# The last four k-tiles of the first layer's shift and scale, summed on VectorE instead of TensorE

## The chip, the cores and the metric

The kernel runs on one core of one Trainium2 chip. The metric is the device time of one execution in microseconds (us), median of the runs shown; the profile is of one further execution. A core has TensorE (PE in the rows; its weight loads are PEld), VectorE (DVE), ScalarE (ACT), GpSimd (POOL) and SyncE (SP), whose queue issues the DMAs that this text is about.

## What is computed

The reference is a two-layer attention block on 256 latent and 256 context tokens of width 2048, followed by one more block (a mixer, a cross-attention and a feed-forward part), all in fp32. The change touches only how each of the first block's two layers gets its modulation. For layer 0:

```python
sc, scc = jax.nn.silu(c), jax.nn.silu(c_ctx)                       # two vectors of 2048
shift, scale, gate = jnp.split(sc @ w_ada[l] + b_ada[l], 3, axis=-1)        # w_ada[l]: 2048 x 6144
shift_c, scale_c, gate_c = jnp.split(scc @ w_ada[l] + b_ada[l], 3, axis=-1)
h = rms(x, norm_w[l]) * (1.0 + scale[:, None]) + shift[:, None]
hc = rms(xc, norm_w[l]) * (1.0 + scale_c) + shift_c
u = h @ w_in[l]                                                    # and hc @ w_in[l]
```

So no product with `w_in` can use a column of `h` before the shift and the scale of that column are there, and these are sums over 2048 rows of `w_ada`.

## The kernel before

**Tiling.** All 512 tokens stand in four tiles of 128 (two latent, two context; t = 0 to 3). The width 2048 is 16 k-tiles of 128 columns. A product with `w_in` for one chunk of 512 output columns, one token tile and one k-tile is three TensorE instructions, since each fp32 factor is split in a rounded part `hi` and a rest `lo` (hi·hi, hi·lo, lo·hi; lines 481 to 483). Weights come by 512 KB loads of two k-tiles (line 448, three `raw` buffers); ScalarE makes each `hi` (line 420) and VectorE each `lo` (line 421), four buffers of each.

**The first products.** `first_products` works through the first three chunks of `w_in` in five parts of the k-tiles, `PARTS`: 0-1, 2-3, 4-7, 8-11, 12-15. I call them parts 0 to 4. In part i all three chunks are multiplied by the k-tiles of that part: 72 products in parts 0 and 1, 144 in each of parts 2 to 4. A chunk has four PSUM banks, one for each token tile, and there are four such banks in all (`psum`, tag d), so a bank is free for the next chunk only when its sums have been moved out: by copies in part 0 (line 408 or 414), by VectorE adds to the earlier parts' sums from part 1 on (line 1403, tiles `va` and `a`).

**Columns of the modulation.** While part i is multiplied, `ada_pe` makes shift and scale of part i+1. It loads the columns of `w_ada` that this part needs (8.4 MB for four k-tiles, 32 loads of 256 KB, line 694; eight buffers, shared tags P and PT) and multiplies them by the two silu vectors, eight groups of four matmuls with 32 columns of weights (line 698, tile `adao`). Its `end` copies the sums out (705), turns them by four transposes (708, `adat`), adds the pieces (712, `adaT`), finishes them (664 to 666) and calls `done`, which makes the next activations: for each k-tile four transposes of x (530), two VectorE multiplications (540, `h`), two ScalarE shifts (543), `hi` (545) and `lo` (546). Two PSUM banks serve these transposes, so the transposes of one k-tile wait until the multiplications of the k-tile two before it are done.

**The other form.** `ada_steps` does such sums on VectorE, for the gates and for layer 1: weights laid out by column, so that a row of 512 products lies in a partition; a step loads two 256 KB tiles (line 736, three `raw2` buffers) and for each of two streams makes one multiplication with a running sum (line 739, SCALAR_TENSOR_TENSOR and a read of the accumulator). The silu vector, spread over all partitions, is a tile `cb` (line 732, two buffers). Before the change this starts after the first products.

**What sets the order.** The program is written in one stream of operations; jobs are taken up by a clock of expected TensorE time (`tick`, `push`, `side_rate`), and a scheduler then puts each engine's instructions in a fixed order. Each engine runs its list strictly in order, and so does SP's queue: an issue that waits for a buffer holds those behind it.

Of the kernel before, what the change touches and what calls it, by code (L numbers as in the profile page):

```python
# [132 lines left out]
def packed_ada(w):  # L133


    x = w[0].reshape(16, 128, 3, D)
    out = [x[:, :, :2, 128 * k0:128 * (k0 + n)].ravel() for k0, n in PARTS]
    for l, a, b in ((0, 2, 3), (1, 0, 2), (1, 2, 3)):
        out.append(w[l][:, a * D:b * D].reshape(4, 512, -1, 128).transpose(0, 2, 3, 1).ravel())
    return np.concatenate(out)  # L140
# [499 lines left out]
class Block1(K):  # L640
# [27 lines left out]
    def ada_pe(self, k0, n, cst, done):  # L668
# [11 lines left out]
        def step(kt0):  # L680
# [15 lines left out]
            for kt, b in reversed(raws):  # L696
                q = 64 * (kt % 2) + 32 * b
                m = nc.tensor.matmul(acc[q:q + 32, :W], lhsT=cst[:, kt, :], rhs=raws[kt, b], start=kt < 2,
                                     stop=kt >= NKT - 2, skip_group_check=True)
                if (kt, b) != (kt0 + 1, 1):  # L700
                    self.tc.keep_in_program_order(m)
# [16 lines left out]
    def ada_steps(self, l, b0, nb, streams):  # L718
# [3 lines left out]
        w, ns, n = self.a["w_ada"], len(streams), 16 * nb  # L722
        st = {}
        at0 = w.offset + ((0 if l == 0 else 16) + (0 if l == 0 else 16 * b0)) * D * 128 + 2 * D * D
# [19 lines left out]
        def end():  # L744
            t = self.ada_tile(l)
            for b in range(nb):
                nc.vector.tensor_reduce(t[:, b0 + b, :ns], st["p"][:, :, 16 * b:16 * b + 16], op=OP.add, axis=AX.X)
            if b0 == 0:
                self.finish_ada(l, 0, 16)
# [632 lines left out]
    def first_products(self, h, w, chunks):  # L1382
# [4 lines left out]
        def steps(i):  # L1387
            k0, n = PARTS[i]

            def done():  # L1390
                h.limit = k0 + n
                h.need(k0 + 1)
            return self.ada_pe(k0, n, self.cst, done)

        h.need(1)
        self.side_rate = self.rates["first"]
        for i, (k0, n) in enumerate(PARTS):
            if i + 1 < len(PARTS):
                for f in steps(i + 1):
                    self.push(f)  # L1400
            self.every = n * len(chunks) * 2.56 / FIRST
# [6 lines left out]
    def block1(self):  # L1408
        nc, a, tc = self.nc, self.a, self.tc
        with ExitStack() as es:  # L1410
# [19 lines left out]
            self.cst = self.B("cstat", tag="cb").rearrange("p (k m) -> p k m", m=32)  # L1430
            nc.vector.memset(self.cst, 0.0)
            nc.vector.tensor_copy(self.cst[:, :, 0:2], self.cv.rearrange("p s k -> p k s"))
# [32 lines left out]
            self.rates = dict(first=0, vb=0.2, b=0.2, z=0.2, cq=0.2, ckv=0.2, c=0, out=0.2)  # L1465
# [537 lines left out]
```

## Time and profile before

| | us |
|---|---|
| median of 3 runs | 3488.35 |
| lowest, highest | 3487.48, 3488.5 |
| the profiled execution | 3488.5 |
| its span in the profile | 3486.4 |
| part 0 to part 4 of the first products, in the span | 35.4 to 219.0 |

The span leaves out 2.1 us of the execution's time around it. In rows of the timeline the columns are the start, the length, the engine, the line, the operation, the tiles (written<-read), the shape and the count, and in brackets the idle time before and what ended it. In a table of stretches each engine has its busy time and its count of instructions; then come the granted TensorE clock (1.00 is 2.4 GHz), the mean busy share of the 16 DMA engines and what they moved in GB/s. Consecutive instructions overlap, so what one costs in a row of its kind is the distance between two starts.

### The profile page before, as it was taken

The page shows a single profiled execution, that of the slowest core. Times are in us where ns is not written, and L with a number is a line of the kernel's source. Part 1 is how long each engine was busy: PE and PEld are TensorE (multiplying, and loading weights), DVE is VectorE, ACT ScalarE, POOL GpSimd, SP SyncE. Part 2 cuts the span into 40 slices and gives each one's busy share as a digit, 9 for nine tenths or more (in the row PEclk, how much of TensorE's full clock was granted, in tenths as well). Part 3 has the DMA queues.
Part 4 walks back from the last instruction along what each step waited for, and adds up shares of the span by engine and source line. Part 5 has one row for each costly group of instructions (what it writes and reads, how often), then busy time and mean ns, then how long its engine had stood idle before and what let it go on. Part 6 is the DMA issues. An engine that isn't in the chain of part 4 may idle for free. (4 is left out here: it accounts for less than half of the span.)

```text
span 3486.4 us, 57207 instructions
## 1 busy us (share of the span) xinstructions
PE 3360.5 (96%) x20842; PEld 2937.7 (84%) x20842; DVE 2296.0 (66%) x4939; ACT 1786.5 (51%) x3556; POOL 318.3 (9%) x472
## 2 busy tenths in 40 slices
PE   7999999999999998999999999999999899999998
PEld 4577778788787887887778999999888899999886
DVE  3488988778866576887664555555666766666554
ACT  3345655246335355756464445444556555555544
POOL 0022220112120121021200000000000000000000
PEclk9999999999999999999999999999999999999999
DMA  8845445642565434444644535555655455555554
GB/s 305 279 125 150 132 142 150 201 133 85 179 212 159 162 96 146 141 157 129 187 135 158 187 122 182 183 185 184 197 179 168 146 183 184 184 182 194 193 192 164
DMA packets 226778, 590.46 MB, mean 169 GB/s; under 512 B 39904, under 2 KB 63184, under 8 KB 226496
## 3 DMA queue, kind: packets, MB, share of 16 engines
q1 hardware_dynamic: 221104, 570.41, 51.2%
q0 software_dynamic: 4864, 15.69, 1.4%
q8 instruction: 164, 2.69, 0.3%
q14 instruction: 118, 0.97, 0.1%
q10 hardware_dynamic: 528, 0.71, 0.1%
HBM read 582.48 MB, written 4.24 MB: 168 GB/s over the span
## 5 line engine op out<-in xcount | busy, mean ns | idle before, releaser
L421 DVE TENSOR_TENSOR lo<-raw,hi 128x512 fp32r<-128x512 f32 (+3 forms) x1788 | 1206.3, 679 | 867.1 <-ACT hi L420 859.5
L420 ACT ACTIVATE hi<-raw 128x512 fp32r<-128x512 f32 (+3 forms) x1788 | 1089.7, 614 | 1254.3 <-PE upd L504 192.6
L502 PE MATMUL upd<-hi,hi 128*128 128x256 f32 x1408 | 399.1, 284 | 0.0
L504 PE MATMUL upd<-lo,hi 128*128 128x256 f32 x1408 | 398.9, 283 | 0.0
L505 PE MATMUL upd<-hi,lo 128*128 128x256 f32 x1408 | 398.7, 283 | 0.0
L739 DVE SCALAR_TENSOR_TENSOR scr<-raw,cb 128x512 f32<-128x512 f32 x448 | 298.2, 691 | 34.9 <-DMA raw<-in_w_ada_dram 17.6
L504 PEld LDWEIGHTS upd<-lo,hi 128*128 128x128 f32 x1408 | 270.7, 192 | 0.3 <-DVE lo L546 0.3
L505 PEld LDWEIGHTS upd<-hi,lo 128*128 128x128 f32 x1408 | 270.6, 192 | 0.0
L502 PEld LDWEIGHTS upd<-hi,hi 128*128 128x128 f32 x1408 | 270.6, 192 | 0.0
L399 POOL TENSOR_TENSOR sm<-sm,mhalf 128x2 f32<-128x2 f32 (+4 forms) x116 | 117.2, 1012 | 1407.4 <-DVE sm L398 1402.0
L481 PE MATMUL downd<-hi,hi 128*128 128x512 f32 x352 | 137.7, 391 | 0.0
L483 PE MATMUL downd<-hi,lo 128*128 128x512 f32 x352 | 137.7, 391 | 0.0
L482 PE MATMUL downd<-lo,hi 128*128 128x512 f32 x352 | 137.6, 391 | 0.0
L602 ACT ACTIVATE P<-Ss,sm 128x512 f32<-128x512 f32 (+1 forms) x164 | 99.6, 608 | 69.2 <-DVE sm L598 51.1
L408 ACT ACTIVATE PT<-pTt 128x256 f32<-128x256 f32 x226 | 79.3, 381 | 64.5 <-PE pTt L619 55.2
L481 PE MATMUL L0outd<-hi,hi 128*128 128x512 f32 x256 | 101.2, 395 | 4.3 <-DVE ot L1361 3.0
L502 PE MATMUL L0zd<-hi,hi 128*128 128x512 f32 x256 | 100.6, 393 | 1.4 <-DVE kpe L414 1.4
L505 PE MATMUL L0zd<-hi,lo 128*128 128x512 f32 x256 | 100.4, 392 | 1.0 <-DVE lo L421 0.9
L598 DVE TENSOR_REDUCE sm<-Ss 128x1 f32<-128x512 f32 (+1 forms) x164 | 95.1, 585 | 7.8 <-PE Ss L591 6.8
L483 PE MATMUL L0outd<-hi,lo 128*128 128x512 f32 x256 | 99.8, 392 | 0.3 <-DVE lo L421 0.3
L482 PE MATMUL L0outd<-lo,hi 128*128 128x512 f32 x256 | 100.0, 391 | 0.0
L504 PE MATMUL L0zd<-lo,hi 128*128 128x512 f32 x256 | 100.0, 391 | 0.0
(568 smaller groups left out, 8920.1 us busy)
## 6 DMA issues: line engine op xcount, KB each, us to landing
raw<-in_w_in_dram SPq DMA_DIRECT2D x344, 512.0 KB, 3.5
raw<-in_w_ada_dram SPq DMA_DIRECT2D x384, 256.0 KB, 3.4
raw<-in_ffn_w_up_dram SPq DMA_DIRECT2D x176, 512.0 KB, 3.5
raw<-in_w_out_dram SPq DMA_DIRECT2D x104, 512.0 KB, 4.1
raw<-in_ffn_w_down_dram SPq DMA_DIRECT2D x88, 512.0 KB, 3.8
raw<-in_w_proj_b_dram SPq DMA_DIRECT2D x32, 512.0 KB, 3.5
raw<-in_w_in_dram SPq DMA_DIRECT2D x32, 288.0 KB, 3.3
raw<-in_w_proj_a_dram SPq DMA_DIRECT2D x16, 512.0 KB, 3.7
```

What stands on the lines that cost most here:

```text
L399: nc.gpsimd.tensor_tensor(r, ms, self.mhalf[:, :n], op=OP.pow)
L420: self.nc.scalar.activation(hi, src, AF.Copy)
L421: self.nc.vector.tensor_sub(lo, src, hi.bitcast(F32))
L481: nc.tensor.matmul(ps[t][:, a], lhsT=xh, rhs=hi[:, a], start=first, stop=False)
L482: nc.tensor.matmul(ps[t][:, a], lhsT=xh, rhs=lo[:, a], start=False, stop=False)
L483: nc.tensor.matmul(ps[t][:, a], lhsT=xl, rhs=hi[:, a], start=False, stop=last)
L502: nc.tensor.matmul(p, lhsT=hi[:, s], rhs=xh, start=kt == 0 and c % per == 0, stop=False, skip_group_check=True)
L504: nc.tensor.matmul(p, lhsT=hi[:, s], rhs=xl, start=False, stop=False, skip_group_check=True)
L505: nc.tensor.matmul(p, lhsT=lo[:, s], rhs=xh, start=False, stop=kt == nk - 1, skip_group_check=True)
L598: nc.vector.tensor_reduce(nm[:, 0:1], S[:, :nk], op=OP.max, axis=AX.X, negate=True)
L602: nc.scalar.activation(P[:, :nk], S[:, :nk], AF.Exp, bias=nm[:, 0:1], accum_out=nm[:, 1:2])
L739: nc.vector.scalar_tensor_tensor(self.temp("scr"), raw, 1.0, st[s], op0=OP.mult, op1=OP.mult, accum_out=st["p"][:, s, k, q:q + 1])
```

## The change

Shift and scale of part 4 (k-tiles 12 to 15) are no longer made by `ada_pe` during part 3 but by `ada_steps`: `packed_ada` lays their weights out by column, `ada_steps` gets a first k-tile `k0` and a call `done`, and its 16 steps run as side work at a rate of 0.2 a microsecond of the clock from part 0 on; what is left of them is issued in one go at the start of part 3, except the last, which follows 20 us later and calls `done`. The constant `cst` becomes two tiles under another tag, because `cb` now holds the silu vectors from the start.

```diff
@@ packed_ada
     x = w[0].reshape(16, 128, 3, D)
-    out = [x[:, :, :2, 128 * k0:128 * (k0 + n)].ravel() for k0, n in PARTS]
-    for l, a, b in ((0, 2, 3), (1, 0, 2), (1, 2, 3)):
-        out.append(w[l][:, a * D:b * D].reshape(4, 512, -1, 128).transpose(0, 2, 3, 1).ravel())
+    out = [x[:, :, :2, 128 * k0:128 * (k0 + n)].ravel() for k0, n in PARTS[:-1]]
+    k0 = PARTS[-1][0]
+    for y in (w[0][:, 2 * D:], w[1][:, :2 * D], w[1][:, 2 * D:], x[:, :, :2, 128 * k0:].reshape(D, -1)):
+        out.append(y.reshape(4, 512, -1, 128).transpose(0, 2, 3, 1).ravel())
     return np.concatenate(out)
@@ ada_steps
-    def ada_steps(self, l, b0, nb, streams):
+    def ada_steps(self, l, b0, nb, streams, k0=0, done=None):
-        w, ns, n = self.a["w_ada"], len(streams), 16 * nb
+        nk = 16 - k0
+        w, ns, n = self.a["w_ada"], len(streams), nk * nb
         st = {}
-        at0 = w.offset + ((0 if l == 0 else 16) + (0 if l == 0 else 16 * b0)) * D * 128 + 2 * D * D
+        at0 = w.offset + 2 * D * 128 * PARTS[-1][0]
+        at0 += D * 128 * (64 if k0 else 0 if l == 0 else 16 + 16 * b0)
@@ ada_steps, end
-                nc.vector.tensor_reduce(t[:, b0 + b, :ns], st["p"][:, :, 16 * b:16 * b + 16], op=OP.add, axis=AX.X)
+                nc.vector.tensor_reduce(t[:, b0 + b, :ns, k0:], st["p"][:, :, nk * b:nk * b + nk], op=OP.add, axis=AX.X)
             if b0 == 0:
-                self.finish_ada(l, 0, 16)
+                self.finish_ada(l, k0, nk)
+                if done:
+                    done()
@@ first_products
-            return self.ada_pe(k0, n, self.cst, done)
+            if i + 1 < len(PARTS):
+                return self.ada_pe(k0, n, self.cst, done)
+            return self.ada_steps(0, 0, 2, [0, 1], k0, done)

         h.need(1)
         self.side_rate = self.rates["first"]
+        later, self.side = self.side, steps(len(PARTS) - 1)
+        last = self.side.pop()
         for i, (k0, n) in enumerate(PARTS):
-            if i + 1 < len(PARTS):
+            if i + 2 < len(PARTS):
                 for f in steps(i + 1):
                     self.push(f)
+            elif self.side is not later:
+                self.flush_side()
+                self.push(20.0)
+                self.push(last)
+                self.side = later
+                self.side_rate = 0
@@ block1
-            self.cst = self.B("cstat", tag="cb").rearrange("p (k m) -> p k m", m=32)
-            nc.vector.memset(self.cst, 0.0)
-            nc.vector.tensor_copy(self.cst[:, :, 0:2], self.cv.rearrange("p s k -> p k s"))
+            self.cst = []
+            for i in range(2):
+                x = self.B("cstat", tag="cqx", bufs=4, cols=256).rearrange("p (k m) -> p k m", m=32)
+                nc.vector.memset(x, 0.0)
+                nc.vector.tensor_copy(x[:, :, 0:2], self.cv[:, :, 8 * i:8 * i + 8].rearrange("p s k -> p k s"))
+                self.cst.append(x)
-            self.rates = dict(first=0, vb=0.2, b=0.2, z=0.2, cq=0.2, ckv=0.2, c=0, out=0.2)
+            self.rates = dict(first=0.2, vb=0.2, b=0.2, z=0.2, cq=0.2, ckv=0.2, c=0, out=0.2)
```

**Where the instructions come to stand.** The line numbers of the changed kernel are two to six, later sixteen, higher in this region (540 is 542, 739 is 743, 1403 is 1419). On TensorE the eight groups, the four transposes and their copy are gone from part 3. Elsewhere the order moves too; two places matter.

The first is VectorE's list around the start of part 3, after the multiplications for k-tiles 8 and 9. Before, these rows lead from k-tile 9 to k-tile 10 (`h_1284` is k-tile 10; `a_154` to `a_157` are the adds that empty the four banks of part 2's last chunk):

```order
L540 SCALAR_TENSOR_TENSOR h_1138<-trs_1133,adaT_77_283,rb_290 128x256 x2
L546 TENSOR_TENSOR lo_1131<-h_1125,hi_1130 128x512
L421 TENSOR_TENSOR lo_1193<-raw_1190,hi_1192 128x512
L546 TENSOR_TENSOR lo_1144<-h_1138,hi_1143 128x512
L421 TENSOR_TENSOR lo_1209<-raw_1190,hi_1208 128x512
L1403 TENSOR_TENSOR a_154_564<-a_154_564,L0firstd_1150 128x512
L1403 TENSOR_TENSOR a_155_566<-a_155_566,L0firstd_1151 128x512
L1403 TENSOR_TENSOR a_156_568<-a_156_568,L0firstd_1152 128x512
L421 TENSOR_TENSOR lo_1235<-raw_1232,hi_1234 128x512
L1403 TENSOR_TENSOR a_157_570<-a_157_570,L0firstd_1153 128x512
L421 TENSOR_TENSOR lo_1276<-raw_1232,hi_1275 128x512
L540 SCALAR_TENSOR_TENSOR h_1284<-trs_1279,adaT_77_283,rb_290 128x256 x2
```

In the changed kernel the same stretch, from k-tile 9 (`h_1274`) to k-tile 10 (`h_1459`), holds 20 of the 64 new multiplications, eight `lo`, the four adds, one reduction and one small add. Its middle, with the second to fourth of the adds (`a_177` to `a_179`):

```order
L743 SCALAR_TENSOR_TENSOR scr_1330,adaP_405<-raw_387_1326,cb_1169 128x512
L423 TENSOR_TENSOR lo_1357<-raw_1338,hi_1356 128x512
L743 SCALAR_TENSOR_TENSOR scr_1368,adaP_405<-raw_395_1366,cb_1167 128x512
L743 SCALAR_TENSOR_TENSOR scr_1370,adaP_405<-raw_395_1366,cb_1169 128x512
L743 SCALAR_TENSOR_TENSOR scr_1374,adaP_405<-raw_398_1372,cb_1167 128x512
L743 SCALAR_TENSOR_TENSOR scr_1376,adaP_405<-raw_398_1372,cb_1169 128x512
L1419 TENSOR_TENSOR a_177_610<-a_177_610,L0firstd_1287 128x512
L1419 TENSOR_TENSOR a_178_612<-a_178_612,L0firstd_1288 128x512
L1419 TENSOR_TENSOR a_179_614<-a_179_614,L0firstd_1289 128x512
L423 TENSOR_TENSOR lo_1435<-raw_1432,hi_1434 128x512
L743 SCALAR_TENSOR_TENSOR scr_1394,adaP_405<-raw_403_1392,cb_1388 128x512
```

and its end:

```order
L423 TENSOR_TENSOR lo_1513<-raw_1480,hi_1512 128x512
L751 TENSOR_REDUCE adaT_78_286<-adaP_405 128x2x4
L668 TENSOR_TENSOR adaT_78_286<-adaT_78_286,vt 128x2x4
L743 SCALAR_TENSOR_TENSOR scr_1418,adaP_405<-raw_415_1416,cb_1388 128x512
L743 SCALAR_TENSOR_TENSOR scr_1420,adaP_405<-raw_415_1416,cb_1390 128x512
L743 SCALAR_TENSOR_TENSOR scr_1424,adaP_405<-raw_418_1422,cb_1388 128x512
L743 SCALAR_TENSOR_TENSOR scr_1426,adaP_405<-raw_418_1422,cb_1390 128x512
L542 SCALAR_TENSOR_TENSOR h_1459<-trs_1454,adaT_78_286,rb_293 128x256 x2
```

So five whole steps of the new sums have moved in between k-tiles 9 and 10, and eight of their multiplications stand ahead of the add that empties the second bank. On TensorE 24 products with k-tiles 8 and 9 stand between the start of part 3 and the first product with k-tile 10, before and after; the transposes of part 3's columns (`adat`) stand 48 products ahead of the end of part 2 before, 27 after.

The second place is SP's queue in part 1. The sixth load of `w_in` (the second half of part 1 needs it) stands before behind eight of the 32 loads of part 2's columns:

```order
L694 DMA raw_602<-in_w_ada_dram 128x512
L694 DMA raw_604<-in_w_ada_dram 128x512
L448 DMA raw_679<-in_w_in_dram 128x1024
L694 DMA raw_619<-in_w_ada_dram 128x512
L694 DMA raw_621<-in_w_ada_dram 128x512
```

and in the changed kernel behind twenty of them and behind a step's pair of the new loads:

```order
L696 DMA raw_709<-in_w_ada_dram 128x512
L740 DMA raw_210_715<-in_w_ada_dram 128x512
L740 DMA raw_213_721<-in_w_ada_dram 128x512
L450 DMA raw_735<-in_w_in_dram 128x1024
L696 DMA raw_747<-in_w_ada_dram 128x512
```

So the load moved back in the queue by twelve column loads and the new pair. Ahead of the last column load of part 2 stand in all four of the new pairs and one pair of `cb`; ahead of the seventh load of `w_in`, the first that part 2 needs, one more pair of each.

## Rows read from the trace of the kernel before

**Rows 1.** Stretches: parts 0, 1, 2 and 3 of the first products.

```profile
35.40:58.90 23.50, 23.48 (x140) 14.59 (x140) 8.61 (x20) 12.09 (x24) 0.00 (x0) 1.00 0.81 274
58.90:93.70 34.80, 29.77 (x158) 15.53 (x156) 17.73 (x33) 8.74 (x17) 0.00 (x0) 0.96 0.81 272
93.70:139.60 45.90, 45.55 (x224) 30.33 (x221) 21.10 (x39) 13.22 (x25) 0.00 (x0) 0.96 0.88 300
139.60:185.00 45.40, 44.19 (x229) 29.64 (x228) 23.01 (x41) 13.56 (x25) 3.26 (x4) 1.00 0.69 224
```

**Rows 2.** Timeline of TensorE in parts 2 and 3: column transposes, groups, products.

```profile
127.20 0.60 PE L708 MATMUL adat<-ident,ada 128*128 128x128 f32 x4
127.64 1.04 PE L530 MATMUL trs<-ident,x 128*128 128x128 f32 x8
...
147.45 1.07 PE L698 MATMUL adao<-raw,cstat 128*32 128x512 f32 x8 [1.21 <-DMA raw<-in_w_ada_dram]
...
150.61 0.40 PE L482 MATMUL L0firstd<-lo,hi 128*128 128x512 f32 x1
150.85 0.40 PE L483 MATMUL L0firstd<-hi,lo 128*128 128x512 f32 x1
151.18 1.06 PE L698 MATMUL adao<-raw,cstat 128*32 128x512 f32 x8
152.17 0.50 PE L481 MATMUL L0firstd<-hi,hi 128*128 128x512 f32 x1
152.51 0.39 PE L482 MATMUL L0firstd<-lo,hi 128*128 128x512 f32 x1
```

**Rows 3.** Timeline of TensorE at the end of part 1: a wait and what follows.

```profile
86.54 0.60 PE L708 MATMUL adat<-ident,ada 128*128 128x128 f32 x4
91.44 0.45 PE L530 MATMUL trs<-ident,x 128*128 128x128 f32 x1 [4.30 <-DVE h L540]
91.82 1.94 PE L698 MATMUL adao<-raw,cstat 128*32 128x512 f32 x8
...
97.91 0.39 PE L483 MATMUL L0firstd<-hi,lo 128*128 128x512 f32 x1
```

**Rows 4.** Stretches of 10 us: around that wait, and after the first products.

```profile
80.00:90.00 10.00, 6.66 (x37) 3.33 (x35) 4.18 (x12) 2.90 (x5) 0.00 (x0) 1.00 1.00 359
90.00:100.00 10.00, 8.56 (x33) 3.81 (x34) 4.06 (x8) 2.86 (x6) 0.00 (x0) 0.66 0.61 201
...
230.00:240.00 10.00, 10.00 (x51) 8.45 (x50) 10.00 (x28) 3.70 (x7) 2.25 (x3) 1.00 0.70 202
```

**Rows 5.** Timeline of VectorE: column sums, activations, adds, multiplications with sum, `lo`.

```profile
127.99 0.25 DVE L712 TENSOR_REDUCE adaT<-adat 128x8 f32<-128x16 f32 x2
...
129.63 1.65 DVE L540 SCALAR_TENSOR_TENSOR h<-trs,adaT,rb 128x256 f32<-128x256 f32 x4
...
144.89 0.88 DVE L540 SCALAR_TENSOR_TENSOR h<-trs,adaT,rb 128x256 f32<-128x256 f32 x2 [3.37 <-PE trs L530]
...
195.08 1.88 DVE L1403 TENSOR_TENSOR va<-va,L0firstd 128x512 f32<-128x512 f32 x3 [0.59 <-PE L0firstd L483]
...
231.18 0.68 DVE L739 SCALAR_TENSOR_TENSOR scr<-raw,cb 128x512 f32<-128x512 f32 x1
...
233.63 1.28 DVE L421 TENSOR_TENSOR lo<-raw,hi 128x512 fp32r<-128x512 f32 x2
```

**Rows 6.** Timeline of ScalarE: the `hi` of k-tile 10.

```profile
146.35 0.63 ACT L545 ACTIVATE hi<-h 128x512 fp32r<-128x512 f32 x1
```

**Rows 7.** Timeline of SP's queue in parts 0 and 1.

```profile
53.67 0.38 SPq L448 DMA_DIRECT2D raw<-in_w_in_dram  x1
60.20 20.37 SPq L694 DMA_DIRECT2D raw<-in_w_ada_dram  x24
80.66 0.85 SPq L448 DMA_DIRECT2D raw<-in_w_in_dram  x2
```

**Rows 8.** The page, DMA issues: size and median time to landing.

```profile
raw<-in_w_ada_dram SPq DMA_DIRECT2D x384, 256.0 KB, 3.4
```

More of the change, by code (lines that the diff above doesn't have):

```diff
@@ L697, in step @@
                 q = 64 * (kt % 2) + 32 * b
-                m = nc.tensor.matmul(acc[q:q + 32, :W], lhsT=cst[:, kt, :], rhs=raws[kt, b], start=kt < 2,
+                m = nc.tensor.matmul(acc[q:q + 32, :W], lhsT=cst[kt // 8][:, kt % 8, :], rhs=raws[kt, b], start=kt < 2,
                                      stop=kt >= NKT - 2, skip_group_check=True)
```

## The prediction

> **What bounds the kernel now.** I read the stretches of the first products first. TensorE is busy nearly throughout parts 0, 2 and 3, VectorE for 8.61 + 17.73 + 21.10 + 23.01 = 70.5 of 149.6 us, the DMA engines for 0.69 to 0.88 [rows 1]. So these parts are bound by TensorE's list, and the column work of the modulation is part of it. Then TensorE's own timeline: products start 0.24 us apart (150.61, 150.85; nearer 0.23 over a longer run), and a column group pushes the next two apart, from 150.85 to 152.17 and 152.51 [rows 2]. The one long wait in part 1 shows what else can bound: after the last columns of part 2 TensorE stands for 4.30 us, released by VectorE's `h` [rows 3], and in that stretch VectorE is busy for only 4.18 of 10 us [rows 4]. What counts there is the place of an instruction in VectorE's list, not VectorE's load. The profiled execution took 3488.5 us (span 3486.4), 0.15 above the median; I count from it.
>
> **What the change takes away.** Part 3 loses eight groups. One costs 152.51 - 150.85 less two product distances of 0.23, so 1.20; eight cost 9.6. The four transposes take 127.64 - 127.20 = 0.44, and the one wait for column loads 1.21 [rows 2]. Together **11.25 us** of TensorE's path. Their loads move to the new steps byte for byte.
>
> **What it adds, by load.** 64 multiplications with a sum. Four start in 233.63 - 231.18 = 2.45, so 0.61 each, accumulator read included [rows 5]; 64 are 39 us. With these VectorE has 109.5 us of work in the 138 us that would be left: it fits, and by load alone it costs nothing. The eight `cb` tiles add 2.1 MB of DMA. Parts 0 to 3 move 39.9 MB (GB/s times length) [rows 1]; 42 MB at the 359 GB/s of a full stretch [rows 4] are 117 us, so this fits too. What covers the new work is idle time of in-order lists, and the cover is gone wherever a needed instruction stands behind it.
>
> **Part 3, by place.** Let 0 be the start of the column transposes for part 3. TensorE: 0.44, then 27 products of part 2 (6.2), so part 3 starts at 6.6; eight transposes of x (about 0.8) and 24 products (5.5) with k-tiles 8 and 9, and at 12.9 it wants k-tile 10. VectorE: the reduction starts 127.99 - 127.20 = 0.8 later, and the fourth `h` ends 131.28 - 127.99 = 3.3 after that [rows 2, 5], at 4.1. Then come 20 of the new multiplications (12.2), eight `lo` and four adds at 0.60 each (two `lo` 1.28 long together, three adds 1.88) [rows 5], 7.2, and some 0.3 of small ones: the `h` of k-tile 10 starts at 23.8. From its start to the end of its `hi` are 146.98 - 144.89 = 2.1 [rows 5, 6]. TensorE gets k-tile 10 at 25.9, not 12.9: it waits **13.0 us**. It stands in two pieces: the add that frees the second bank ends after eight multiplications and six other rows, at 4.1 + 4.9 + 3.6 = 12.6, while TensorE asks at 8.8 after the six products of the first bank (3.8 of waiting); the remaining 9.2 come ahead of k-tile 10. Behind the new multiplications wait the `lo` and the adds, and for these TensorE. If the reduction is late as well, the wait grows one for one; if TensorE reaches this place late and VectorE doesn't, it shrinks. I keep 9 to 16.
>
> Two smaller prices belong to it. After the 4.30 us wait the granted clock of the next 10 us is 0.66 [rows 4], part of it at the level of 1.2 instead of 2.4 GHz: a group takes 1.94 instead of 1.06, and from 91.82 to 97.91 [rows 3] run two groups and five products, which at full clock take 3.6; that is 2.5 lost. For two waits I take 3.5, between 0 and 5. And the new multiplications themselves can wait for data: three buffers, 3.4 us from issue to landing [rows 8], and a fresh pair of `cb` that can be asked for only when the old pair is used up. Ten loads in 3.4 us turns of three are 11 us, within the 20, so I take 1, at most 3. Part 3 in sum: -11.25 + 13.0 + 3.5 + 1 = **+6.25** (-2 to +13).
>
> **Parts 0 to 2, by place.** The end of part 0: the column transposes had 18 products behind them as cover and now have 5, with eight transposes of x right after, which wait for the fourth `h`. That `h` comes at 4.1 as above, the cover is about 1.4: +2.5 (0 to 3). Part 1: the sixth load of `w_in` was issued at 53.67, before the 24 loads that took until 80.57 to issue [rows 7]; now twenty of the 32 column loads and a new pair are ahead of it. SP's queue stops behind each load whose buffer TensorE hasn't yet freed, so it lands about when it is needed: +1.5 (0 to 4). The DMA engines have less slack here than elsewhere: 15.9 MB in parts 0 and 1 [rows 1], ten loads more (2.6 MB) ahead of the last columns, 51.6 us at 359 GB/s out of 58.3. The end of part 1: the 4.30 us wait is there in any case; one more step, 2.4 us of VectorE, now stands ahead of the reduction, with its two loads and two `cb` ahead of the seventh load of `w_in`: +2.5 (0 to 5). Part 2 holds 20 of the new multiplications, 12.2 us beside 21.1 busy of 45.9 [rows 1]; I find none ahead of something late and take 0 (0 to 3). Sum **+6.5** (0 to 13). Part 4 and all that follows have the same work in the same order, bound by TensorE, so the delay is handed on; the two smaller `cst` tiles cost nothing that anyone waits for.
>
> **Sum.** 3488.5 + 6.25 + 6.5 = **3501 us**.
>
> **The rivals.** (a) *Load decides, and the change wins.* VectorE has room, so the new work is swallowed, the wait at k-tile 10 dissolves because VectorE has run ahead, and the part boundaries cost 2: 3488.5 - 11.25 + 2 = 3479. For it: at 230 to 240 us VectorE is busy for 10.00 of 10 and TensorE for 10.00 too [rows 4]. Against it: the 4.30 us wait beside an idle VectorE, and that VectorE can't run ahead, since the rows in question stand behind `h` of k-tiles 8 and 9. It decides if the new multiplications between `h` of 9 and of 10 are done within 9 us. The Trainium skill (Perfetto Trace Analysis, Identifying the Most-Contended Engine) takes occupancy as a fair measure of how near VectorE is to its limit; by that rule a VectorE at 109.5 of 138 us is no bound and this rival is right, while the trace's wait beside a VectorE at 4.18 of 10 speaks against reading it so. I give (a) 0.10. (b) *A wash.* Boundaries cost 2 and the wait is 9 with no loss of clock: 2 - 11.25 + 9 + 0 = about 0, 3488; with any mixture within 7 us either way 0.25. (c) *The queue.* DMAs in parts 0 and 1 run full, each late load stops SP's queue, every group of part 1 waits as the one at 147.45 did (1.21), 8 x 1.21 = 10 on top of the forecast: 3511 and more; 0.07. That the sums are not moved at all is out: the order shows them gone from TensorE's list.
>
> **How the numbers follow.** The forecast, slower by 7 to 22, has 0.58, (c) 0.07, (b) 0.25, (a) 0.10. A measurement of this kernel can tell about 0.2%, 7 us, from no change. So faster 0.10, the same 0.25, slower 0.65. The range goes from 3486, the low ends of both sums (-2 and 0), to 3511, which is 10 above the forecast and takes in most of the high ends; about 0.1 lies below it and 0.07 above.
>
> **What would show it.** In the changed profile: no column groups between the start of part 3 and its end; VectorE's list without a gap from the `h` of k-tile 9 to that of k-tile 10 and some 20 us long; TensorE waiting there first for an add (the second bank) and then for `h` of k-tile 10, 13 us together, with a granted clock well below 1 behind it; part 2 starting some 6 us later than at 93.7, part 4 some 13 later than at 185.0, and 34 us long as now. I am wrong if TensorE passes from k-tile 9 to 10 without a wait of several us, or if part 2 starts on time.

## The result

The changed kernel is slower: a median of 3518.51 us (3514.69 to 3521.36, four runs) against 3487.91 of the kernel before on the same chip; the ratio is 1.0087, with a 95% interval of 1.0075 to 1.0099. The profiled execution took 3514.69 us with a span of 3512.6, which is 26.2 more than the span before. The first product after the five parts (`L0vbd`) starts at 243.25 instead of 220.0: 23.3 of the 26.2 us arise ahead of it, 22.3 in the five parts and 1.0 before part 0.

The stretches of the five parts in the changed kernel, columns as in [rows 1], which they answer:

```profile
36.40:63.06 26.66, 25.41 (x148) 15.37 (x146) 13.20 (x36) 12.13 (x24) 0.00 (x0) 1.00 0.85 297
63.06:108.60 45.54, 31.91 (x149) 17.97 (x148) 24.39 (x58) 7.16 (x15) 0.00 (x0) 0.83 0.74 238
108.60:157.10 48.50, 47.19 (x220) 29.36 (x221) 31.51 (x79) 13.35 (x27) 0.00 (x0) 0.98 0.88 304
157.10:208.30 51.20, 38.66 (x161) 30.67 (x160) 40.28 (x90) 13.36 (x25) 3.63 (x4) 0.90 0.52 163
208.30:242.30 34.00, 34.00 (x153) 27.48 (x152) 21.70 (x39) 12.43 (x22) 6.95 (x4) 1.00 0.23 78
```

In part 3 TensorE is busy for 38.66 us instead of 44.19, and the part is still 5.8 longer. The larger loss is in part 1: 45.5 us instead of 34.8, with TensorE busy for 31.91.

**Part 1.** SP's queue there (start, time until the last of the group was issued, line, operation, tiles, count; line 450 loads `w_in`, 696 columns for TensorE, 740 weights of the new steps, 736 the silu tile `cb`), to be held against [rows 7]:

```profile
56.73 18.98 SPq L696 DMA_DIRECT2D raw<-in_w_ada_dram  x14
75.81 0.85 SPq L740 DMA_DIRECT2D raw<-in_w_ada_dram  x2
76.76 0.58 SPq L450 DMA_DIRECT2D raw<-in_w_in_dram  x1
78.22 14.66 SPq L696 DMA_DIRECT2D raw<-in_w_ada_dram  x12
92.97 0.86 SPq L736 DMA_DIRECT2D cb<-silu  x2
93.89 0.90 SPq L740 DMA_DIRECT2D raw<-in_w_ada_dram  x2
94.88 1.41 SPq L450 DMA_DIRECT2D raw<-in_w_in_dram  x1
```

The sixth load of `w_in`, issued at 53.67 before, goes out at 76.76, 13.7 us after the start of part 1. The last pair of new weights of part 1 is asked for at 93.89, behind twelve column loads. What waits for it, in the timelines of TensorE, ScalarE and VectorE (the dots mark rows left out):

```profile
81.45 1.07 PE L700 MATMUL adao<-raw,cstat 128*32 128x512 f32 x8 [1.51 <-DMA raw<-in_w_ada_dram]
84.74 2.07 PE L483 MATMUL L0firstd<-hi,hi 128*128 128x512 f32 x4 [2.23 <-ACT hi L422]
...
96.93 1.06 PE L700 MATMUL adao<-raw,cstat 128*32 128x512 f32 x8 [1.72 <-DMA raw<-in_w_ada_dram]
103.38 1.11 PE L710 MATMUL adat<-ident,ada 128*128 128x128 f32 x4 [5.39 <-ACT ada L707]
106.64 1.94 PE L532 MATMUL trs<-ident,x 128*128 128x128 f32 x8 [2.15 <-DVE h L542]
```

```profile
84.06 1.15 ACT L422 ACTIVATE hi<-raw 128x512 fp32r<-128x512 f32 x2 [19.08 <-DMA raw<-in_w_in_dram]
102.73 0.60 ACT L707 ACTIVATE ada<-adao 128x512 f32<-128x512 f32 x1 [17.52 <-DVE scr L743]
```

```profile
101.30 0.69 DVE L743 SCALAR_TENSOR_TENSOR scr<-raw,cb 128x512 f32<-128x512 f32 x1 [5.37 <-DMA raw<-in_w_ada_dram]
...
104.53 0.26 DVE L714 TENSOR_REDUCE adaT<-adat 128x8 f32<-128x16 f32 x2
```

Read from below: VectorE stands idle for 5.37 us until the pair has landed, at 101.30. ScalarE's `ada`, the copy of the column sums that TensorE finished at 98.0, waits for the multiplications on that pair, though it reads nothing of them: `scr` (a multiplication's unused product), `ada` and `h` share three scratch buffers, handed round in program order, and the next one is held by a late `scr`. So the transposes of part 2's columns start at 103.38 after 5.39 of waiting, then the reduction, and the `h` that [rows 3] shows behind a wait of 4.30. Earlier, `hi` of the late `w_in` load costs 2.23. With 0.61 at 77.06, the waits of part 1 are 13.6 us, before 4.8 (4.30 and 0.49).

There may be a second reason for the lateness besides the place in the queue: two `cb` tiles were issued just ahead of the pair, at 92.97. From 97.0 to 100.5, shortly before the pair has landed, the DMA engines are 0.98 busy and move only 238 GB/s, where [rows 4] has 359 at a share of 1.00:

```profile
97.00:100.50 3.50, 0.99 (x8) 0.08 (x8) 0.00 (x0) 0.00 (x0) 0.00 (x0) 0.92 0.98 238
```

In the like stretches of e1, e3 and e4 below it is 240 to 288 at shares of 0.95 to 1.00. So these tiles seem to cost the DMA engines more than their bytes say; no run took them away alone, and how much of the 5.37 us is theirs stays open.

**Part 3.** TensorE and VectorE (answers to [rows 2, 5]):

```profile
164.00 0.50 PE L483 MATMUL L0firstd<-hi,hi 128*128 128x512 f32 x1 [3.37 <-DVE a L1419]
...
178.33 1.51 PE L532 MATMUL trs<-ident,x 128*128 128x128 f32 x6 [8.36 <-DVE h L542]
```

```profile
163.27 1.87 DVE L1419 TENSOR_TENSOR a<-a,L0firstd 128x512 f32<-128x512 f32 x3
...
167.95 0.69 DVE L743 SCALAR_TENSOR_TENSOR scr<-raw,cb 128x512 f32<-128x512 f32 x1 [0.63 <-DMA cb<-silu]
...
177.31 1.65 DVE L542 SCALAR_TENSOR_TENSOR h<-trs,adaT,rb 128x256 f32<-128x256 f32 x4
```

These are the two waits of the prediction: first for the add of the second bank, then for `h` of k-tile 10, which starts 22.9 us after that of k-tiles 8 and 9 ended (it starts at 152.74 and is 1.66 us long in the same timeline).

### The profile page after: what moved, and what is told of

Read it like the earlier page. It is cut to its first block, busy times and chain, and to the rows that moved or that the text cites. A ratio compares the mean times of both kernels' runs of the same rounds, so it can differ in the third digit from the quotient of the medians.

```text
span 3512.6 us, 57235 instructions
## 1 busy us (share of the span) xinstructions
PE 3366.6 (96%) x20774; PEld 2947.0 (84%) x20774; DVE 2338.0 (67%) x5069; ACT 1783.7 (51%) x3555; POOL 320.0 (9%) x472
## 5 line engine op out<-in xcount | busy, mean ns | idle before, releaser
L743 DVE SCALAR_TENSOR_TENSOR scr<-raw,cb 128x512 f32<-128x512 f32 x512 | 343.7, 699 | 48.7 <-DMA raw<-in_w_ada_dram 27.4
```

The lines of the kernel that those rows point to most:

```text
L743: nc.vector.scalar_tensor_tensor(self.temp("scr"), raw, 1.0, st[s], op0=OP.mult, op1=OP.mult, accum_out=st["p"][:, s, k, q:q + 1])
```

## The experiments

Parts are in us of one profiled execution each; the column "start" is where part 0 begins, the next to last where `L0vbd` starts, against 220.0. Where a matmul record is missing, a boundary is off by up to 0.5 us. Behind `L0vbd` the traces differ by up to 12 us (3260.6 to 3272.9 to the end of the span, 3266.4 before) for no reason that I can name, and the plain runs of one kernel by as much; so I judge by the parts and give the median beside them (before: 3487.1 to 3489.9 in the runs that these were compared with). The two measures can differ: by the median e6 loses 25.7 us and e8 5.1. How far to trust the parts shows in e4: up to part 3 its lists are those of the changed kernel, and its parts 0 to 2 came out 3.1 us longer. Differences of 3 us between two traces are not read as effects here.

| kernel | start | 0 | 1 | 2 | 3 | 4 | `L0vbd` against before | median, ratio to before (95%) |
|---|---|---|---|---|---|---|---|---|
| before | 35.4 | 23.5 | 34.8 | 45.9 | 45.4 | 34.0 | 0 | |
| changed | 36.4 | 26.7 | 45.5 | 48.5 | 51.2 | 34.0 | +23.3 | 3518.5, 1.0075 to 1.0099 |
| e1 short sums | 35.3 | 26.4 | 46.0 | 49.8 | 44.1 | 34.3 | +16.8 | 3508.9, 1.0031 to 1.0061 |
| e2 no new loads | 35.8 | 26.0 | 36.1 | 46.1 | 42.5 | 34.0 | +1.4 | 3495.1, 1.0003 to 1.0022 |
| e9 neither | 35.5 | 25.5 | 37.0 | 44.0 | 35.4 | 34.2 | -7.5 | 3484.0, 0.9981 to 1.0003 |
| e5 sums left out | 35.6 | 24.6 | 34.0 | 45.1 | 34.7 | 34.0 | -11.1 | 3476.7, 0.9960 to 0.9978 |
| e3 own scratch | 36.0 | 27.6 | 43.8 | 49.2 | 40.2 | 34.3 | +12.0 | 3506.3, 1.0026 to 1.0055 |
| e4 spread in part 3 | 35.4 | 27.2 | 46.9 | 49.7 | 43.7 | 34.2 | +18.0 | 3504.2, 1.0021 to 1.0050 |
| e7 late start | 35.7 | 23.2 | 35.0 | 50.6 | 43.9 | 46.3 | +15.6 | 3507.7, 1.0039 to 1.0078 |
| e8 late, own scratch | 35.3 | 24.2 | 35.3 | 55.6 | 48.1 | 35.0 | +13.3 | 3492.7, 1.0001 to 1.0026 |
| e6 GpSimd's queue | 41.1 | 24.1 | 36.0 | 52.5 | 45.4 | 34.0 | +14.0 | 3513.3, 1.0057 to 1.0092 |
| e11 GpSimd, held | 35.6 | 23.6 | 39.3 | 52.1 | 45.8 | 34.0 | +11.3 | 3505.9, 1.0029 to 1.0059 |
| e10 GpSimd, held, own scratch | 35.5 | 26.9 | 42.5 | 52.5 | 34.7 | 34.0 | +7.0 | 3500.0, 1.0021 to 1.0045 |
| e12 own scratch, no loads | 36.4 | 27.3 | 34.5 | 44.4 | 34.7 | 34.0 | -7.7 | 3484.0, 0.9981 to 1.0003 |

### VectorE's time or the data: e1, e2, e9, e5

e1, the 64 multiplications on 16 columns instead of 512:

```diff
-nc.vector.scalar_tensor_tensor(self.temp("scr"), raw, 1.0, st[s], ...
+c = 16 if k0 else 512
+nc.vector.scalar_tensor_tensor(self.temp("scr")[:, :c], raw[:, :c], 1.0, st[s][:, :c], ...
```

> The changed kernel with each of the 64 new multiplications cut to 16 of its 512 columns (most of the sum is left out): all loads, waits, buffers and places in the lists stay, only VectorE's time of 39 us goes. Theory 1 (place and lateness: part 1 is long because the new loads land late and other things stand behind the instructions that wait for them; part 3 because 12 us of multiplications stand ahead of k-tile 10): part 1 stays 42 to 46 us long, part 3 loses its waits of 3.4 and 8.4 us and the clock behind them, about 14 us, to 37; about 3504 us. Rival 1 (VectorE's time itself is what costs, everywhere): part 1 goes back to 35 or 36 as well; about 3490. Rival 2 (only the longer DMA queue costs, in parts 0 to 2): part 1 stays, part 3 stays at 51; about 3517.

Part 1 stayed long, as expected. Part 3 did not come back to 37: it took 44.1, and the wait for `h` of k-tile 10 was still there, though the new multiplications took next to no time. TensorE, then VectorE ahead of that `h`:

```profile
172.03 1.51 PE L532 MATMUL trs<-ident,x 128*128 128x128 f32 x6 [8.35 <-DVE h L542]
```

```profile
163.46 0.17 DVE L744 SCALAR_TENSOR_TENSOR scr<-raw,cb 128x16 f32<-128x16 f32 x1 [1.07 <-DMA cb<-silu]
...
165.55 0.18 DVE L744 SCALAR_TENSOR_TENSOR scr<-raw,cb 128x16 f32<-128x16 f32 x1 [1.90 <-DMA cb<-silu]
...
168.66 0.18 DVE L744 SCALAR_TENSOR_TENSOR scr<-raw,cb 128x16 f32<-128x16 f32 x1 [1.42 <-DMA raw<-in_w_ada_dram]
...
170.82 0.17 DVE L744 SCALAR_TENSOR_TENSOR scr<-raw,cb 128x16 f32<-128x16 f32 x1 [1.27 <-DMA raw<-in_w_ada_dram]
...
171.01 1.65 DVE L542 SCALAR_TENSOR_TENSOR h<-trs,adaT,rb 128x256 f32<-128x256 f32 x4
```

The transfers alone take nearly as long as the multiplications did: from the end of `h` of k-tile 9 to `h` of k-tile 10 pass 18.6 us, 22.9 in the changed kernel. My theory 1 had the place right and the resource only half right. The wait for the add is gone.

e2, the data taken away and VectorE's time left:

```diff
 for s in streams:
+    if k0 and q:
+        continue
     st[s] = self.B("cb")
...
-raw = self.B("raw2", bufs=3)
-nc.sync.dma_start(raw, ...
+if not k0 or q == i == 0:
+    raw = st["r", k % 2] = self.B("raw2", bufs=3)
+    nc.sync.dma_start(raw, ...
+raw = st["r", k % 2] if k0 else raw
```

> The changed kernel with the loads of the 16 new steps taken away but for the first pair of weights and of the silu tile, which all steps read (the sums are of the wrong weights): VectorE's 64 multiplications stay, 7.9 MB of weights and 1.6 MB of silu tiles are not loaded. Theory 1: part 1 goes back from 45.6 to 35 to 38 us, since nothing that stands behind a multiplication waits for data any more; part 3 keeps its wait at k-tile 10 of 8 to 12 us, unless more of the steps have been done before it; about 3508. Rival 1 (VectorE's time): part 1 stays at 43 or more; about 3517. Rival 2 (only the queue): parts 0 and 1 as before the change and also part 3 shorter by its waits, about 3490.

Part 1 is back at 36.1 as expected. Nearly everything else is too: `L0vbd` 1.4 late instead of 23.3. Part 3 still waits, less than expected:

```profile
143.96 0.47 PE L483 MATMUL L0firstd<-hi,hi 128*128 128x512 f32 x1 [1.54 <-DVE a L1423]
155.09 1.09 PE L532 MATMUL trs<-ident,x 128*128 128x128 f32 x4 [4.58 <-DVE h L542]
```

The same twenty multiplications stand between k-tiles 9 and 10, but VectorE begins them earlier: 48 of the 64 lie before part 3, 42 in the changed kernel.

e9 is both edits together, e5 the sums left out of the kernel before:

```diff
+if i + 1 == len(PARTS):
+    def only():
+        self.nc.vector.memset(self.ada_tile(0)[:, 0:2, :, k0:], 0.0)
+        done()
+    return [20.0, only]
 return self.ada_pe(k0, n, self.cst, done)
```

> e1 and e2 together: the 64 new multiplications are cut to 16 columns each and the new steps load nothing but the first pair (sums wrong and mostly left out). The instructions, their scratch buffers and their places remain, neither VectorE's time nor the data. Theory 1 (each of the two alone is enough to hold up k-tile 10 in part 3: in e1 the data, 8.35 us, in e2 VectorE's time, 1.54 and 4.58 us): with both gone part 3 takes 34 to 36 us without a wait over 1.5, parts 0 to 2 come out within 4 us of before, and the time is about 3479. A rival (an order fixed by the scratch buffers is enough by itself): part 3 keeps a wait of 4 us or more for h of k-tile 10, about 3487.

> The kernel before with shift and scale of the last four k-tiles not summed at all (set to zero), neither on TensorE nor on VectorE, and their 32 loads gone. It bounds what the change could gain. If TensorE's list is what sets the end of part 3, as the prediction's first sum has it, part 3 goes from 45.7 to 34 to 35 us and the time falls by 11 to 12, to 3477. A rival (TensorE only waits elsewhere, for adds or for k-tiles, once it is faster): part 3 at 40 or more, 3483 or more.

Both came as expected: part 3 takes 35.4 and 34.7 us without a wait over 0.5. Its stretch in e9:

```profile
142.00:177.40 35.40, 35.19 (x162) 28.35 (x161) 23.85 (x55) 13.32 (x25) 0.00 (x0) 1.00 0.38 122
```

From the four corners of e1, e2, e9 and the change: the data cost 24.3 us without VectorE's time (-7.5 to +16.8) and 21.9 with it (+1.4 to +23.3); VectorE's time costs 8.9 without the data and 6.5 with them. The scheduler fills the lists anew for each of these kernels, so every price includes the order that came with it. The twenty multiplications between k-tiles 9 and 10 stand there in e9 too: that order is not enough by itself.

### Where and when the steps run: e3, e4, e7, e8

e3 gives the unused products their own buffer:

```diff
+if k0 and q == i == 0:
+    st["scr"] = self.temp("scr", tag="rb", bufs=2)
...
-nc.vector.scalar_tensor_tensor(self.temp("scr"), raw, ...
+nc.vector.scalar_tensor_tensor(st["scr"] if k0 else self.temp("scr"), raw, ...
```

> The changed kernel with one change: the new multiplications write their unused products to a buffer of their own instead of one of the three scratch buffers that they share with ada (ScalarE's copy of the column sums) and h. Loads, their order and the number of instructions stay. Theory 1 in its narrow form (the wait of 5.39 us ahead of the column transposes of part 2 comes from ada waiting for a scratch buffer that a late multiplication holds): this wait goes, part 1 is 5 to 7 us shorter (39 to 41), the waits of 2.2 us for hi and of 0.6 to 1.7 us for column loads stay; part 3 within 3 us of 51; about 3511. Rival 2 (the queue alone; the copy would be late anyhow): part 1 stays at 44 to 46; about 3518.

The wait for `ada` fell from 5.39 to 0.80, but part 1 got only 1.7 shorter, no more than two traces of the same lists differ by, because the next instruction that needs VectorE waited instead:

```profile
98.83 1.11 PE L710 MATMUL adat<-ident,ada 128*128 128x128 f32 x4 [0.80 <-ACT ada L707]
105.43 1.73 PE L532 MATMUL trs<-ident,x 128*128 128x128 f32 x7 [5.48 <-DVE h L542]
```

```profile
99.99 0.26 DVE L714 TENSOR_REDUCE adaT<-adat 128x8 f32<-128x16 f32 x2 [4.71 <-PE adat L710]
101.08 0.69 DVE L745 SCALAR_TENSOR_TENSOR scr<-raw,cb 128x512 f32<-128x512 f32 x1 [0.83 <-DMA raw<-in_w_ada_dram]
...
104.80 1.26 DVE L542 SCALAR_TENSOR_TENSOR h<-trs,adaT,rb 128x256 f32<-128x256 f32 x3
```

Four multiplications on the late pair now lie between the reduction and the last `h`. So the scratch buffers were one way for the lateness to reach TensorE, not its cause. What I had not expected is part 3, 11 us shorter: without the shared buffers the scheduler puts `h` of k-tile 10 ahead of most of the multiplications and single ones between the adds (its list from k-tile 9 to k-tile 10 holds eight of the new multiplications instead of twenty).

e4 spreads what was issued in one go at the start of part 3:

```diff
-last = self.side.pop()
...
-elif self.side is not later:
-    self.flush_side()
-    self.push(20.0)
-    self.push(last)
+elif i + 1 == len(PARTS):
+    self.flush_side()
```

> The changed kernel with one change: what is left of the new steps at the start of part 3 is not issued in one go there but goes on at the rate of 0.2, and what is still left then at the start of part 4. Parts 0 to 2 are the same, instruction for instruction. Theory 1: the waits of 3.37 and 8.36 us in part 3 shrink to 2 to 4 in all, with the clock behind them; part 3 goes from 51 to 38 to 41 us, and part 4 may start up to 3 us late; about 3507. A rival (the wait only moves: VectorE is then late at the end of part 3, or the adds wait instead): part 3 and 4 together stay within 3 us of 85; about 3518.

Part 3 got 7.5 us shorter, not 10 to 13: the 3.37 for the add stayed, the wait for k-tile 10 fell from 8.36 to 1.74. Parts 0 to 2, the same instructions in the same order, end 19.6 late (17.5 in the changed kernel).

e7 is e4 with a start in part 2 (the side rate set only for parts 2 and 3, 0.25), e8 adds the own buffer at a rate of 0.35.

> The changed kernel with the new steps started only in part 2, at a rate of 0.25, and not issued in one go at the start of part 3; what is left is issued at the start of part 4. Parts 0 and 1 then have no new load and no new multiplication in SP's and VectorE's lists. Theory 1: parts 0 and 1 as before (23 and 35 us), part 2 up to 4 us longer, part 3 between 36 and 42, part 4 up to 4 us later for the last step; about 3490. A rival (the new loads cost the same wherever they are put): parts 2 to 4 together 10 us or more longer than before; about 3500.

> As e7_late_start, at a rate of 0.35 and with the own buffer for the unused products of e3. Theory 1: parts 0 and 1 as before, the multiplications lie one by one between the others, part 2 up to 2 us longer, part 3 35 to 38 us, part 4 on time; about 3481, faster than both kernels. A rival (three buffers for the new weights on SP's queue still delay w_in's loads): parts 2 and 3 together stay over 90 us; 3488 or more.

Parts 0 and 1 are as before in both, so what they lost was due to the early start. But the loss went along with the steps, as the rivals said: e7 lost 12 us in part 4, where what was left of the sums made TensorE wait 8.76 for `h`, and e8 10 us in part 2 (3.42 for a `hi` of `w_in`, 2.13 for column loads) and 3 in part 3.

### The queue or the bytes: e6, e11, e10, e12

e6 issues the new loads from GpSimd's queue (`nc.gpsimd` in place of `nc.sync` for steps with `k0`). e11 also holds the first three weight loads and two silu tiles back, by one-column copies on GpSimd that wait for the columns of part 0 (the lines for the silu tiles are left out here); e10 adds e3's buffer to e11:

```diff
...
+if k0 and q == 0 and 2 * i + k % 2 < 3:
+    nc.gpsimd.tensor_copy(raw[:, 0:1], self.ada_tile(0)[:, 0, 0, 0:1])
-nc.sync.dma_start(raw, ...
+(nc.gpsimd if k0 else nc.sync).dma_start(raw, ...
```

> The changed kernel with one change: the loads of the 16 new steps (weights and silu tiles) are issued from GpSimd's queue instead of SP's. All bytes are still moved and all 64 multiplications stay in VectorE's list, which the scheduler now fills as in the kernel without the new loads (e2). SP's queue is again in the order of the kernel before. Theory 1, after e1 to e3 (what is late are transfers, because SP's queue stops at each load whose buffer is not free and the new and old loads hold each other up): parts 0 to 2 are back within 3 us of before, 23, 35 and 46, part 3 takes 34 to 38, the waits at k-tile 10 are under 3 us; about 3482. A rival (the bytes: the DMA engines are full in parts 0 and 1, and 9.4 MB more there delay everything, whatever queue asks): parts 0 and 1 together stay over 66 us, and the end of part 4 is 10 us or more later than before; about 3500.

> e10 without the own buffer: loads on GpSimd's queue, the first ones held back, the unused products again in the three scratch buffers shared with ada and h. Theory 1: start as before, parts 0 and 1 within 2 us of before, part 2 50 to 53 and part 3 45 as in e6 (wait of 8 us for h of k-tile 10), about 3503; so that against e10 it shows what the shared scratch buffers cost by the order that they force. A rival (scratch buffers don't matter once the queue is another): as e10 within 4 us.

> The changed kernel with three changes: the new loads on GpSimd's queue (e6), the own buffer for the unused products (e3), and the first three weight loads and the first two silu loads held back by one-column copies on GpSimd until the columns of part 0 are finished, so that they don't meet the loads of x. In VectorE's list all multiplications now stand ahead of the h of part 3. Theory 1: start as before (35.4), parts 0 and 1 within 2 us of before, part 3 34 to 36 us; part 2, which then moves more bytes, decides: 46 to 54; about 3482, with luck faster than the kernel before by what can be measured. A rival (the bytes: with 8.4 MB more in parts 0 to 2, 40 MB in 104 us or 386 GB/s, something there is late whatever queue asks): parts 0 to 2 together 12 us or more over the 104 of before; 3489 or more.

e6 started 5.7 us late: GpSimd has nothing to wait for and asks for the first weights at 1.35 and for the other four of its first five loads at 13.48 to 15.67, among the loads of x, in a stretch (0 to 41.1) where the DMA engines are 0.95 busy. Its parts 0 and 1 were back at 60.1 together (before 58.3, changed 72.2), with data that had partly come before. e11 starts on time, and parts 0 and 1 take 62.9. Its SP queue, for [rows 7] and the rows of the result:

```profile
54.40 0.42 SPq L450 DMA_DIRECT2D raw<-in_w_in_dram  x1
60.91 24.50 SPq L696 DMA_DIRECT2D raw<-in_w_ada_dram  x24
```

The sixth load of `w_in` is at its old place and time. So with the new loads on another queue 9.3 of the 13.9 us lost in parts 0 and 1 are back (VectorE's list, which the scheduler fills anew, is not quite the same). Part 3 of e11 (45.8, a wait of 9.04 for `h` of k-tile 10) against that of e10 (34.7, no wait over 1) is the price of the shared scratch buffers and of the order that comes with them: twenty of the multiplications stand between k-tiles 9 and 10 in e11, none in e10. Most of these 11.1 us only move, since parts 0 to 2 of e10 are 6.9 longer than those of e11; at `L0vbd` the two are 4.3 apart, little more than the rival of e11 allowed. For e10 loses in parts 0 to 2, 121.9 us against 104.2 before. Its first three parts:

```profile
35.50:62.40 26.90, 24.50 (x141) 14.75 (x139) 19.03 (x51) 11.61 (x23) 6.11 (x12) 1.00 1.01 360
62.40:104.90 42.50, 33.29 (x158) 16.81 (x158) 30.83 (x75) 8.86 (x18) 6.43 (x12) 0.90 0.89 305
104.90:157.40 52.50, 47.56 (x224) 30.90 (x221) 38.82 (x99) 13.21 (x25) 9.08 (x16) 0.95 0.86 301
```

The DMA engines are full in part 0 (1.01, 360 GB/s), and in part 1 TensorE waits 6.4 us for column loads. The three parts move 38.5 MB (GB/s times length), 29.7 before; by my estimate at the 360 GB/s of part 0 38.5 MB take 107 us, more than the 104.2 that there were, though less than the 121.9 that it took.

> The changed kernel with the own buffer for the unused products (e3) and without the new steps' loads but for the first pair of weights and silu tiles (e2; the sums are of the wrong weights). VectorE's list is close to that of e10: nearly all 64 whole multiplications lie ahead of the h of part 3, in parts 0 to 2. Against e10 only the bytes are gone. If the bytes made the 18 us that parts 0 to 2 of e10 are longer than before, these parts come back to 104 to 107 us, part 3 stays 34 to 35, part 4 ends 6 to 10 us earlier than before, about 3480. If VectorE's lists made them (39 us of multiplications between the adds and lo that TensorE waits for), parts 0 to 2 stay at 112 or more and the time is 3488 or more.

e12 is e3 and e2 together. Its parts 1 to 3:

```profile
63.70:98.20 34.50, 28.07 (x150) 15.09 (x146) 30.22 (x77) 6.98 (x14) 0.00 (x0) 0.99 0.85 290
98.20:142.60 44.40, 44.40 (x219) 30.20 (x217) 39.52 (x100) 13.33 (x25) 0.95 (x1) 0.97 0.81 266
142.60:177.30 34.70, 34.70 (x161) 28.47 (x160) 21.84 (x36) 13.32 (x25) 2.21 (x3) 1.00 0.34 107
```

Without the loads parts 0 to 2 take 106.2 us and `L0vbd` starts 7.7 early, 14.7 before e10. VectorE is as full as in e10 (39.52 of 44.4 in part 2) and TensorE does not wait there. So the loads decide, not VectorE's time. Which side of them, the bytes on full DMA engines or the waits for single loads to land, e12 does not tell apart, since it takes away both; the bytes alone, at 107 us, would make 2.8 of the 17.7. The Trainium skill (DMA: Bandwidth & Descriptors, Issuing engines are not separate DMA queues) says that transfers asked for by any engine run on the same 16 DMA engines; e10, with loads from two queues and a DMA share of 1.01 in part 0, agrees. It also says that several issuing engines save only the time of issuing; here e11 disagrees, since on one queue a load that waits for its buffer holds those behind it, and another queue gave 9.3 us back.

No version that was run with all of the sums and loads beats the kernel before. I see none that would, which is argued and not run: the 8.4 MB of weights must come either in parts 0 to 2, where e10 found no room for them, or in part 3, where VectorE would have 39 us of multiplications beside its 23 busy in 45.4. Fewer k-tiles moved, or more than three buffers for the new weights, were not tried.

## Why the prediction was right and wrong

The direction was right, the size was not: 3501 was forecast with a range to 3511, and 3518.5 measured. By the steps of the prediction, in us of the profiled executions:

| step | forecast | measured |
|---|---|---|
| TensorE's work gone from part 3 | -11.25 | -10.7 in part 3 of e5, -11.1 in all |
| waits in part 3 | 13.0 | 12.5 (0.81, 3.37, 8.36) |
| clock and data in part 3 | +4.5 | +4.0 (what is left of its sum) |
| part 3 in sum | +6.25 | +5.8 |
| part 0 | +2.5 | +3.2 |
| part 1 | +4.0 | +10.7 |
| part 2 | 0 | +2.6 |
| start | 0 | +1.0 |
| part 4 | 0 | 0 |
| behind part 4 | 0 | +2.9 |

**Right: what is taken away, and the place in part 3.** e5 confirms the first sum (11.25) within 0.6. The two waits of part 3 stand where the prediction put them, 3.37 and 8.36 for 3.8 and 9.2, and behind the multiplications that the prediction named.

**Right only in size: the reason in part 3.** The prediction gave the 13 us to VectorE's time and 1 us to the data. e1 takes VectorE's time away and the wait for `h` of k-tile 10 stays at 8.35; e2 takes the data away and 6.1 of waiting stays. Each alone is enough for about half of it or more, so the good sum for part 3 is partly luck. The step on data went wrong in "3.4 us from issue to landing" [rows 8], which is a median over the whole span. From 35 to 140 us the changed kernel's own loads had

```profile
raw<-in_w_ada_dram SPq DMA_DIRECT2D x89, 256.0 KB, 5.1
raw<-in_w_in_dram SPq DMA_DIRECT2D x9, 512.0 KB, 5.9
cb<-silu SPq DMA_DIRECT2D x4, 256.0 KB, 6.4
```

(size and median time to landing). The same stretch of the kernel before would have shown 4.7 for the columns.

**Wrong: part 1, and with it the argument by load.** "42 MB at the 359 GB/s of a full stretch [rows 4] are 117 us, so this fits too" averaged over four parts of which one has the room: before the change parts 0 to 2 move 274, 272 and 300 GB/s and part 3 224 [rows 1], and the change takes the loads out of part 3 and puts most of them ahead of it (24 of the 32 are issued before 157.1). The step that failed is the price of part 1, +1.5 for the sixth load and +2.5 for the end of the part: for these 4.0 us 10.7 were measured, 8.8 of it more waiting and some 2 the half clock behind the wait at 84.74 (eleven products from 84.74 to 89.60, 0.44 us apart instead of 0.23). I counted the multiplications ahead of the reduction (2.4 us of VectorE) and saw the two loads in SP's queue, but did not ask when these land: the sixth load lands late enough for `hi` to cost 2.23 us, and the pair is issued at 93.89, behind twelve column loads that move only as TensorE frees their buffers, and VectorE stood for 5.37 us. That the scratch buffers lead this wait on to `ada` was not seen at all, though three tiles of one tag stand in the code; by e3 this way of the lateness was worth little, since `h` waited in its place. That the data are the cause of part 1 is shown by e1, where it stays at 46.0 without VectorE's time, and e2, where it takes 36.1 without the data.

**The rivals.** (a) was refuted for this kernel, but e12 shows its condition: with the data there and the unused products in a buffer of their own, VectorE at 132 busy of 175 us holds TensorE up no more than before the change (the longest wait is 3.12 us for `h` at the end of part 1, 4.30 before). The rule of the Trainium skill (Perfetto Trace Analysis, Identifying the Most-Contended Engine), that VectorE's occupancy is a fair measure of how near it is to its limit, agrees with e12 and is no guide to the changed kernel, whose VectorE at 24.39 of 45.5 in part 1 is far from full while TensorE waits for it. The same page of the Trainium skill (Optimization Strategy) says that the most-contended engine can change over time, and that is what [rows 1] by part, read for the DMA engines, would have told. (b), a wash, is out by the measured time. (c), the queue, came nearest to the time and had the smallest chance. Its form was not quite right: the column groups waited 0.6 to 1.7 us, and the larger part of the lateness went through VectorE.

**Open.** The 1.0 us at the start: kernels with the same code there started between 35.3 and 36.4, so I don't count it as the change's. 2.9 of the 26.2 us arise behind the start of `L0vbd`, and the median is 3.8 over the profiled run; both are within what the traces and runs of one kernel differ by, and no run looked for a cause. How much of e3's gain in part 3 is the buffers themselves and how much the other order that the scheduler then chose was not told apart. What the `cb` tiles cost by themselves was not run.

## What to carry to other kernels

Moving work from a full engine to a half idle one moves its loads in time as well: compare the bytes stage by stage with what the DMA engines still have there, and take the landing time from that stage. Follow a new load through its queue: what must be freed before it is issued, what stands behind the instruction that waits for it, and which buffers of the same pool that instruction holds, even one for a result that nobody reads. A wait seen in the trace can have two causes, each enough for it; only taking them away one at a time and both together shows what either is worth.

## What was not expected of the hardware

GpSimd's DMA issues keep GpSimd itself busy: 0.54 us for each in e6, where they are the rows

```profile
13.48 1.14 POOL L736 DMA_DIRECT2D cb<-silu  x2 [1.29 <-DMA silu<-c]
14.61 1.06 POOL L740 DMA_DIRECT2D raw<-in_w_ada_dram  x2
```

and five loads of 256 KB asked for in the first 16 us, 1.3 MB, delayed TensorE's first product by 5.7 us, more than the 3.6 that 1.3 MB take at 360 GB/s by the same estimate. e10 and e11, which hold these loads back, start at 35.5 and 35.6; why the delay is longer than the bytes was not looked into.

In part 3 of the changed kernel a multiplication on VectorE takes longer while GpSimd works on tensors of its own. One of each kind:

```profile
159.71 0.73 POOL L1089 TENSOR_TENSOR H<-H,cs 128x256 f32<-128x256 f32 x1 [129.58 <-DMA H<-in_rp_dram]
159.76 1.22 DVE L743 SCALAR_TENSOR_TENSOR scr<-raw,cb 128x512 f32<-128x512 f32 x1
```

GpSimd has four such instructions there, and each meets a multiplication of 1.20 to 1.23 us, where the others take 0.68 or 0.69. Three of the four stand ahead of `h` of k-tile 10 and lengthen the list there by some 1.6 us.
